# One hybrid decoder layer: the low part of k on both partition halves, and stick-breaking weights as products of sigmoids

## The chip, the core and the metric

The kernel runs on one NeuronCore of a Trainium2 chip. The metric is the device time of one execution in microseconds, lower is better. A NeuronCore has five engines that run their own instruction streams in order: TensorE (PE, with its weight loads shown apart as PEld), VectorE (DVE), ScalarE (ACT), GpSimd (POOL) and SyncE (SP), whose queue issues nearly all DMAs here. They wait for each other by semaphores.

## What is computed

One layer over 512 tokens of width 1024: a SwiGLU sublayer, a mixer of two attention groups side by side (8 heads of 64 each), and a second SwiGLU sublayer. Each is normed before and after and modulated by c. The change lies in the mixer:

```python
p = n @ w_in[l]
qa, ka, va, qi, ki, wi, qb, kb, vb = jnp.split(p, IN_SPLITS, axis=-1)
# group A: an indexer (8 heads qi, one shared ki) picks 128 keys a row; softmax over these
sc = relu(einsum('bthd,bsd->bths', qi, ki));  score = einsum('bths,bth->bts', sc, wi)
_, idx = lax.top_k(score, topk)
# group B: stick-breaking attention, strictly causal
z = jnp.einsum('bthd,bshd->bhts', qb, kb) * (D ** -0.5)
u = jnp.where(mask, jax.nn.log_sigmoid(-z), 0.0)
between = lax.cumsum(u, axis=3, reverse=True) - u
a = jnp.where(mask, jnp.exp(jax.nn.log_sigmoid(z) + between), 0.0)
```

So a[t,s] is sigmoid(z[t,s]) times the product of sigmoid(-z[t,j]) over s < j < t.

## The kernel before

All matrix products run on TensorE in its single-pass float32. To keep accuracy each operand is split into a high and a low part: `split` rounds the source to the high part (ACT, L132) and subtracts it from the source for the low part (DVE or POOL, L138). A projection is then three products per k-tile (L271 to L273: high times low, high times high, low times high), each of 128 rows and 512 columns.

The mixer runs in these stages:

- **Indexer.** `proj_block` (L293) and `proj` make the keys ki and four pairs of heads qi. Then come the scores: for each of 8 heads and token tiles 1 to 3, one q k^T (`qk`, L781) into a PSUM bank (tag `at`, three banks), a Relu on ACT (L734) into one of three buffers, and a weighted sum on DVE (L735).
- **Top-k.** Per row 16 rounds of MAX (L766) and MATCH_REPLACE (L769) on DVE, for three token tiles, then `ns` (L772). Nothing needs it before group A, and the scheduler strews it over DVE's stream among the work of group B.
- **Group B**, four units of two heads: `attn_b` makes the weights x, `transposed` turns them by PE and splits them (ACT, DVE), and `unit` multiplies them with v. Meanwhile `fill` issues the projection of the next unit's k, q and v, step by step.
- **Group A**, four units with `attn_a` in place of `attn_b`: a mask and bias table b (L917), the row maximum (L924), Exp (L927). The output projection's first products fill its last unit.

The order on each engine is fixed when the kernel is built, by a scheduler that goes by the program's order, buffers and its own costs.

How `qk` multiplies is what the first part of the change touches. q's two heads are stacked by `stack` (three SP DMAs of 64 partitions): head 0 has the tile [high; low], head 1 [low; high], and k is stacked as [high; high]. One product of 128 rows (L787) thus gives (q_high + q_low) k_high. The missing term q_high k_low is a product of its own ahead of it (L786), over the 64 partitions on which q_high of that head lies, with `kl`, the split's low part of k, which is not stacked.

`attn_b` per token tile of L = 128 to 512 keys: z in PSUM, with -1e30 added on the diagonal block (L893). ACT makes ln(1 + exp(-|z|)) in three steps (L895 to L897), ACT (tiles 0 and 1, L899) or DVE (tiles 2 and 3, L901) makes max(z, 0), DVE runs the sum of both from the right (the scan, L902), subtracts it from z (L903), and ACT takes Exp (L904). The function table of natural logarithm and exponential is loaded once, in the indexer (L685).

Of the kernel before, what the change touches and what calls it, by code (L numbers as in the profile page):

```python
# [20 lines left out]
S = 512  # L21
# [7 lines left out]
TOPK = 128  # L29
# [25 lines left out]
class Pools:  # L55
    """Work tiles of a phase: 4 KB ones (tag wk) have a pool of their own."""
# [8 lines left out]
class Block:  # L65
    """One launch's context: the tile pools that last, the constants and the parts of the layer."""
# [42 lines left out]
    # ---- pieces  # L109

    def w_load(self, src, view, n=1024, alloc=None, lo=None, hi=None):
        """A block of weights in SBUF, split."""
# [11 lines left out]
    def w_cols(self, w, c0, m, alloc=None, lo=None, hi=None):  # L124
        """Columns c0..c0+m of w [1024, n], as [128, 8, m], split."""
# [3 lines left out]
    def rounded(self, hi, src, eng=None):  # L129
        """src in the tensor engine's single-pass float32."""  # L130
# [4 lines left out]
    def split(self, hi, lo, src, eng=None, hi_eng=None):  # L135
        """src = hi + lo exactly, both in the tensor engine's single-pass float32."""
        a = self.rounded(hi, src, hi_eng)
        return a, (eng or self.nc.vector).tensor_sub(lo, src, hi.bitcast(F32))  # L138
# [36 lines left out]
    def ada_cols(self, m, k0, k1):  # L175
        """What follows from modulation m's columns k0..k1."""
# [11 lines left out]
    def gate_row(self, s, pool):  # L188
        """gate * g_post of sublayer s, on every partition."""
# [5 lines left out]
    def turn(self, src, nk, tp):  # L195
        """src [128 tokens, nk * 128] transposed, four k-tiles a bank."""
# [9 lines left out]
    def to_cols(self, banks, scale_col, shift_col, nh, i, pool):  # L206
        """The banks of turn() scaled and shifted, rounded into token tile i of nh; the rest of it for rest_cols()."""
# [21 lines left out]
    def norm_rows(self, i, pool):  # L229
        """h[i] times its reciprocal root mean square."""  # L230
# [13 lines left out]
    def pre_norm(self, s, n, tp, pool):  # L244
        """The stages of a pre-norm: rows, their transposes, columns."""
# [21 lines left out]
    def mm3(self, ps, w, n, k, m, cols):  # L267
        """The three products of k-tile k that make ps += (w n), w and n split."""
# [6 lines left out]
    def proj(self, w, c0, m, n, psum, lo=None):  # L275
        """(n w[:, c0:c0+m])^T as [m, S] in PSUM."""
# [6 lines left out]
    def proj_block(self, ws, n, banks, ends=()):  # L283
        """Several such products, over the first token tiles before the last ones, whose transposes come meanwhile."""
# [16 lines left out]
    def down_load(self, w, ks, n, half, alloc=None, lo=None):  # L301
        """Half the columns of w's k-tiles ks[n] and ks[n + 1], split: (n, high, low) of each."""
# [5 lines left out]
    def down_mms(self, ps, lhs, ks, i, ck):  # L308
        """Token tile i's products of the k-tiles ck; lhs(k): k-tile k's high and low parts, transposed."""
# [7 lines left out]
    def down(self, lhs, ks, w, g, banks, pool, alloc, stages, begun=0, out=None):  # L317
        """h += g * rmsnorm(lhs^T w), over the k-tiles ks in their order; then each token tile i goes
        through the stages. banks(half): four accumulators; the first half has begun k-tiles in them."""
# [61 lines left out]
    # ---- sublayers  # L381
# [582 lines left out]
```

## Time and profile before

| | |
|---|---|
| median of 3 runs | 1148.08 us (1143.62 to 1151.46) |
| the profiled execution | 1141.3 us from its first to its last instruction; what its own run took around that is not shown apart |
| PE busy | 1089.9 us (95%) |
| PEld busy | 871.1 us (76%) |
| DVE busy | 632.3 us (55%) |
| ACT busy | 434.9 us (38%) |
| POOL busy | 167.7 us (15%) |
| granted TensorE clock, mean | 0.991 of 2.4 GHz |

A busy PE is not yet a PE at its best: matmuls are pipelined, and their records overlap. What a product really costs is the step from its start to the next one's start. In the rows, L12 is line 12 of the kernel; `64*128 64x256` is a product with 64 rows of weights, 128 columns of them, over 256 columns of the other operand; `xN` is a count; in square brackets stand the engine's idle time just before and what ended it. `SPq` is an issue of DMAs.

### The profile page before, as it was taken

The page shows a single profiled execution, that of the slowest core. Times are in us where ns is not written, and L with a number is a line of the kernel's source. Part 1 is how long each engine was busy: PE and PEld are TensorE (multiplying, and loading weights), DVE is VectorE, ACT ScalarE, POOL GpSimd, SP SyncE. Part 2 cuts the span into 40 slices and gives each one's busy share as a digit, 9 for nine tenths or more (in the row PEclk, how much of TensorE's full clock was granted, in tenths as well). Part 3 has the DMA queues.
Part 4 walks back from the last instruction along what each step waited for, and adds up shares of the span by engine and source line. Part 5 has one row for each costly group of instructions (what it writes and reads, how often), then busy time and mean ns, then how long its engine had stood idle before and what let it go on. Part 6 is the DMA issues. An engine that isn't in the chain of part 4 may idle for free.

```text
span 1141.3 us, 13392 instructions
## 1 busy us (share of the span) xinstructions
PE 1089.9 (95%) x5079; PEld 871.1 (76%) x5079; DVE 632.3 (55%) x1055; ACT 434.9 (38%) x790; POOL 167.7 (15%) x116
## 2 busy tenths in 40 slices
PE   3889999999999999999999999989999999999997
PEld 2767888888888887667776677769888888888886
DVE  5979898834223184599999756474333333332313
ACT  3322222223213363477774645555232223321220
POOL 2110000000000433323323320423000000000030
PEclk9889999999999999999999999999999999999999
DMA  9967897732222504322234322412333333322321
GB/s 280 274 203 270 287 303 247 249 100 93 92 93 93 157 20 106 91 75 64 78 87 125 83 84 84 130 55 63 99 98 92 93 105 97 92 92 95 99 84 74
DMA packets 169444, 142.91 MB, mean 125 GB/s; under 512 B 6748, under 2 KB 142076, under 8 KB 169380
## 3 DMA queue, kind: packets, MB, share of 16 engines
q1 hardware_dynamic: 167872, 139.82, 40.2%
q10 hardware_dynamic: 1508, 2.24, 0.6%
q8 instruction: 40, 0.66, 0.2%
q14 instruction: 24, 0.20, 0.1%
HBM read 132.04 MB, written 2.13 MB: 118 GB/s over the span
## 4 chain that ended last, share of the span: by engine, by line
PE 79%; DVE 10%; issue 3%; ACT 2%; SPq 2%; DMA 2%; POOL 1%; DVEq 0%; POOLq 0%; ACTq 0%
PE mm L271 14%; PE mm L273 14%; PE mm L272 14%; PE mm L314 7%; PE mm L315 7%; PE mm L313 7%; PE mm L293 3%; PE mm L466 3%; PE at L787 2%; PE at L786 2%; DVE y L902 1%; DVE h L339 1%; SPq L420 1%; DVE tk L769 1%; PE tp L880 1%
## 5 line engine op out<-in xcount | busy, mean ns | idle before, releaser
L132 ACT ACTIVATE wh<-raw 128x1024 fp32r<-128x1024 f32 x156 | 164.3, 1057 | 450.4 <-PE mm L272 145.7
L271 PE MATMUL mm<-nl,wh 128*128 128x512 f32 x808 | 319.4, 395 | 0.0
L272 PE MATMUL mm<-nh,wh 128*128 128x512 f32 x808 | 316.5, 392 | 0.0
L273 PE MATMUL mm<-nh,wl 128*128 128x512 f32 x808 | 316.4, 392 | 0.0
L138 DVE TENSOR_TENSOR wl<-raw,wh 128x1024 fp32r<-128x1024 f32 (+1 forms) x116 | 142.3, 1227 | 223.3 <-ACT wh L132 223.2
L273 PEld LDWEIGHTS mm<-nh,wl 128*128 128x128 f32 x808 | 151.8, 188 | 30.9
L272 PEld LDWEIGHTS mm<-nh,wh 128*128 128x128 f32 x808 | 152.0, 188 | 28.7
L271 PEld LDWEIGHTS mm<-nl,wh 128*128 128x128 f32 x808 | 152.2, 188 | 28.4
L315 PE MATMUL mm<-wh,hT 128*128 128x512 f32 x352 | 138.6, 394 | 0.0
L314 PE MATMUL mm<-wh,hT 128*128 128x512 f32 x352 | 138.6, 394 | 0.0
L313 PE MATMUL mm<-wl,hT 128*128 128x512 f32 x288 | 113.6, 395 | 0.0
L138 POOL TENSOR_TENSOR wh<-raw,wh 128x1024 fp32r<-128x1024 f32 x10 | 25.5, 2558 | 595.0 <-ACT wh L132 591.8
L138 POOL TENSOR_TENSOR wl<-raw,wh 128x1024 fp32r<-128x1024 f32 x31 | 74.6, 2408 | 164.9 <-ACT wh L132 142.8
L514 DVE TENSOR_TENSOR sg<-sg,mm 128x512 f32<-128x512 f32 x44 | 30.1, 685 | 106.5 <-PE mm L273 91.5
L314 PEld LDWEIGHTS mm<-wh,hT 128*128 128x128 f32 x352 | 66.3, 188 | 15.3
L315 PEld LDWEIGHTS mm<-wh,hT 128*128 128x128 f32 x352 | 66.3, 188 | 15.1
L153 DVE SCALAR_TENSOR_TENSOR acc<-ra,sc,acc 128x1024 f32<-128x1024 f32 x49 | 62.8, 1281 | 5.6 <-DMA ra<-in_w_ada_dram 4.8
L313 PEld LDWEIGHTS mm<-wl,hT 128*128 128x128 f32 x288 | 54.3, 188 | 12.7
L466 PE MATMUL mm<-nh,wh 128*128 128x512 f32 x96 | 35.6, 450 | 6.8 <-ACT nh L445 6.8
L786 PE MATMUL at<-kq 64*128 64x256 f32 (+2 forms) x88 | 37.6, 427 | 2.8 <-DVE mx L924 2.0
L787 PE MATMUL at<-kq 128*128 128x256 f32 (+2 forms) x88 | 38.0, 432 | 0.0
L786 PEld LDWEIGHTS at<-kq 64*128 64x128 f32 x88 | 16.1, 183 | 27.4 <-issue 13.9
(213 smaller groups left out, 1358.1 us busy)
## 6 DMA issues: line engine op xcount, KB each, us to landing
ra<-in_w_ada_dram SPq DMA_DIRECT2D x56, 512.0 KB, 5.1
raw<-in_w_ffn_gate_dram SPq DMA_DIRECT2D x44, 512.0 KB, 3.7
raw<-in_w_ffn_up_dram SPq DMA_DIRECT2D x44, 512.0 KB, 3.7
raw<-in_w_ffn_down_dram SPq DMA_DIRECT2D x44, 512.0 KB, 3.4
raw<-in_w_in_dram SPq DMA_DIRECT2D x28, 512.0 KB, 3.8
ra<-in_w_ada_dram SPq DMA_DIRECT2D x32, 256.0 KB, 5.4
kq<-kq SPq DMA_DIRECT2D x60, 128.0 KB, 2.3
raw<-in_w_out_dram SPq DMA_DIRECT2D x8, 512.0 KB, 3.9
```

Of the source, the lines that this page charges most:

```text
L132: return self.nc.scalar.activation(hi, src, AF.Copy)
L138: return a, (eng or self.nc.vector).tensor_sub(lo, src, hi.bitcast(F32))
L153: nc.vector.scalar_tensor_tensor(acc, raw, sc[:, k:k + 1], acc, op0=ALU.mult, op1=ALU.add)
L271: nc.tensor.matmul(ps[0:m, c], w[0][:, k, :], n[1][:, k, c], start=k == 0, stop=False)
L272: nc.tensor.matmul(ps[0:m, c], w[0][:, k, :], n[0][:, k, c], start=False, stop=False)
L273: return nc.tensor.matmul(ps[0:m, c], w[1][:, k, :], n[0][:, k, c], start=False, stop=k == KD - 1)
L313: nc.tensor.matmul(ps, lh[:, t], wl, start=n == 0, stop=False)
L314: nc.tensor.matmul(ps, ll[:, t], wh, start=False, stop=False)
L315: nc.tensor.matmul(ps, lh[:, t], wh, start=False, stop=n == len(ks) - 1)
L466: nc.tensor.matmul(banks[j], ws[j][l][:, k, :], n[r][:, k, :], start=k + o == 0, stop=k == KD - 1 and o == 2)
L786: nc.tensor.matmul(ps, q[hd][b, t], kl[b, 0:n], start=True, stop=False)
L787: nc.tensor.matmul(ps, q[hd][:, t], k[hd][:, 0:n], start=False, stop=stop)
```

## The change

`qk` takes the low part of k for each head as a tile of its own, over all 128 partitions, so that its first product has 128 rows too; it now also adds q_low k_low. For this `end_k` stacks `kl` as it stacks `kh` (three DMAs and one tile more for each unit of two heads), and the tag `kq` gets 13 buffers in place of 12. In the indexer ki lies on both halves already. Room is made by a bf16 mask `cm` and by `kk` in the ring `w2`.

`attn_b` takes sigmoid(-z) and sigmoid(z) on ACT, runs the product of sigmoid(-z) from the right on DVE (a scan with a broadcast column of ones as its second operand), and multiplies sigmoid(z) with the product one place to the right. The table loaded in the indexer is that of sigmoid; the one with Exp is loaded later, ahead of group A's first Exp.

```diff
     def kq_tile(self, n=2):
-        return [self.upool.tile([128, 512], F32R, tag="kq", name="kq", bufs=12) for _ in range(n)]
+        return [self.upool.tile([128, 512], F32R, tag="kq", name="kq", bufs=13) for _ in range(n)]
...
-        cm = pool.tile([128, 512], F32, tag="cm", name="cm")
+        cm = pool.tile([128, 512], BF16, tag="cm", name="cm")
...
-        load = nc.scalar.preload_act_table_set("natural_log_exp_and_others")
+        load = nc.scalar.preload_act_table_set("sigmoid_and_others")
...
-            kk = pool.tile([128, NT, 64], F32, tag="kk", name="kk")
+            kk = pool.tile([128, NT, 64], F32, tag="w2", name="kk", bufs=3)
...
-                self.qk(ps, i, hd % 2, qi[hd // 2], (kih, kih), kil, True)
+                self.qk(ps, i, hd % 2, qi[hd // 2], (kih, kih), (kil, kil), True)
...
-        t, b = slice(i * 128, (i + 1) * 128), slice(64 * hd, 64 * hd + 64)
-        nc.tensor.matmul(ps, q[hd][b, t], kl[b, 0:n], start=True, stop=False)
+        t = slice(i * 128, (i + 1) * 128)
+        nc.tensor.matmul(ps, q[hd][:, t], kl[hd][:, 0:n], start=True, stop=False)
         nc.tensor.matmul(ps, q[hd][:, t], k[hd][:, 0:n], start=False, stop=stop)
...
         def end_k():
-            kh, st["kl"] = self.kq_tile()
-            self.split(kh, st["kl"], st["ps"])
+            kh, kl = self.kq_tile()
+            self.split(kh, kl, st["ps"])
             st["k"] = self.stack(kh, kh)
+            st["kl"] = self.stack(kl, kl)
...
-            nc.scalar.activation(xs, z, AF.Abs)
-            nc.scalar.activation(xs, xs, AF.Exp, scale=-1.0)
-            nc.scalar.activation(xs, xs, AF.Ln, bias=1.0)
-            if i < 2:
-                nc.scalar.activation(ys, z, AF.Relu)
-            else:
-                nc.vector.tensor_scalar(ys, z, 0.0, None, op0=ALU.max)
-            nc.vector.tensor_tensor_scan(ys[:, ::-1], ys[:, ::-1], xs[:, ::-1], 0.0, op0=ALU.add, op1=ALU.add)
-            nc.vector.tensor_sub(xs, z, ys)
-            nc.scalar.activation(xs, xs, AF.Exp)
+            nc.scalar.activation(ys, z, AF.Sigmoid, scale=-1.0)
+            nc.scalar.activation(xs, z, AF.Sigmoid)
+            nc.vector.tensor_tensor_scan(ys[:, ::-1], ys[:, ::-1], self.ones.to_broadcast([128, L]), 1.0,
+                                         op0=ALU.mult, op1=ALU.mult)
+            nc.vector.tensor_mul(xs[:, 0:L - 1], xs[:, 0:L - 1], ys[:, 1:L])
```

The scheduler also orders the mixer's work anew. Two places show it. First DVE at the end of group B; `tk` and `ns` belong to top-k, `pt` and `v` to a unit's products, `y` and `x` to `attn_b`. Before, the last of top-k stands behind the last weights of group B:

```order
L769 MATCH_REPLACE tk<-m_4912,tk 128x256
L769 MATCH_REPLACE tk<-m_4914,tk 128x384
L769 MATCH_REPLACE tk<-m_4916,tk 128x512
L772 TENSOR_TENSOR ns<-tk,sco 128x256
L772 TENSOR_TENSOR ns<-tk,sco 128x384
L138 TENSOR_TENSOR v<-tp,v 128x8x64
L867 TENSOR_TENSOR ob<-ob,tp 128x4x64
L772 TENSOR_TENSOR ns<-tk,sco 128x512
```

After the change, on the same engine and at the end of the same group, it stands ahead of the last head's weights (the first column of lines is that of the changed kernel: L899 is the scan, L901 the product):

```order
L772 TENSOR_TENSOR ns<-tk,sco 128x384
L138 TENSOR_TENSOR kq<-mm,kq 128x512
L138 TENSOR_TENSOR pt<-tp,pt 128x256
L899 SCALAR_TENSOR_TENSOR y<-y,ones 128x256
L772 TENSOR_TENSOR ns<-tk,sco 128x512
L901 TENSOR_TENSOR x<-x,y 128x255
L899 SCALAR_TENSOR_TENSOR y<-y,ones 128x384
L901 TENSOR_TENSOR x<-x,y 128x383
L899 SCALAR_TENSOR_TENSOR y<-y,ones 128x512
L901 TENSOR_TENSOR x<-x,y 128x511
```

What moved: top-k ends some ten instructions earlier in DVE's stream, with group B's last weights behind it. Second, SP's queue in one unit of group B, with k's stack, the weights `raw` of a later projection, and q's stack. Before (`kq_4600` is k's high part, `kq_4702` and `kq_4703` q's parts):

```order
L778 DMA kq_4604<-kq_4600 64x512 x2
L778 DMA kq_4600<-kq_4600 64x512
L120 DMA raw_5308<-in_w_in_dram 128x8x128
L778 DMA kq_4708<-kq_4702 64x512
L778 DMA kq_4708<-kq_4703 64x512
L778 DMA kq_4702<-kq_4703 64x512
L120 DMA raw_5400<-in_w_in_dram 128x8x128
```

After, in the same queue and unit (`kq_4529` and `kq_4530` are k's high and low parts, `kq_4626` and `kq_4627` q's):

```order
L778 DMA kq_4533<-kq_4529 64x512 x2
L778 DMA kq_4537<-kq_4530 64x512 x2
L120 DMA raw_5224<-in_w_in_dram 128x8x128
L778 DMA kq_4529<-kq_4529 64x512
L778 DMA kq_4530<-kq_4530 64x512
L120 DMA raw_5236<-in_w_in_dram 128x8x128
L778 DMA kq_4632<-kq_4626 64x512
L778 DMA kq_4632<-kq_4627 64x512
L778 DMA kq_4626<-kq_4627 64x512
L120 DMA raw_5332<-in_w_in_dram 128x8x128
```

What moved: three DMAs more stand with k's stack, ahead of the weights and of q's stack.

## Rows read from the trace of the kernel before

**Rows 1.** Busy us (xinstructions) of PE, PEld, DVE, ACT, POOL by stage; then PEclk, DMA share, GB/s
```profile
445.00:486.00 41.00, 41.00 (x154) 26.00 (x152) 21.73 (x25) 16.77 (x32) 14.34 (x8) 1.00 0.43 112
486.00:612.00 126.00, 124.67 (x593) 88.32 (x594) 121.89 (x272) 90.53 (x216) 37.92 (x20) 1.00 0.28 76
612.00:632.00 20.00, 17.60 (x83) 12.51 (x82) 15.67 (x44) 7.94 (x24) 3.61 (x3) 1.00 0.38 118
632.00:735.00 103.00, 98.63 (x483) 74.53 (x483) 63.14 (x162) 56.39 (x127) 32.74 (x18) 1.00 0.35 100
```
**Rows 2.** PE's waits from 445 to 735 us: total us, times, longest us
```profile
PE at L786 <- DVE mx L924: 2.0, 1, 2.0
PE tp L880 <- DVE pt L138: 2.0, 4, 1.4
...
PE at L786 <- DMA kq<-kq: 0.8, 1, 0.8
...
PE tp L863 <- ACT ot L860: 0.2, 1, 0.2
```
**Rows 3.** Timeline of the indexer, one pair of score products: start us, us, what
```profile
446.16 0.19 PEld L273 LDWEIGHTS mm<-nh,wl 128*128 128x128 f32 x1
446.39 0.39 PE L273 MATMUL mm<-nh,wl 128*128 128x512 f32 x1
446.70 0.18 PEld L786 LDWEIGHTS at<-kq 64*128 64x128 f32 x1 [0.36 <-issue]
446.70 0.38 PE L786 MATMUL at<-kq 64*128 64x256 f32 x1
447.01 0.19 PEld L787 LDWEIGHTS at<-kq 128*128 128x128 f32 x1
447.01 0.39 PE L787 MATMUL at<-kq 128*128 128x256 f32 x1
447.24 0.40 PE L271 MATMUL mm<-nl,wh 128*128 128x512 f32 x1
```
**Rows 4.** Timeline, the same around a pair of 512 columns, and L271 to L272
```profile
450.52 0.39 PE L273 MATMUL mm<-nh,wl 128*128 128x512 f32 x1
...
451.60 0.39 PE L271 MATMUL mm<-nl,wh 128*128 128x512 f32 x1
...
451.82 0.40 PE L272 MATMUL mm<-nh,wh 128*128 128x512 f32 x1
```
**Rows 5.** Timeline, eight products of 128 rows and 256 columns, and the next
```profile
425.86 1.12 PE L293 MATMUL mm<-nh,wl 128*128 128x256 f32 x8
426.82 0.28 PE L293 MATMUL at<-nh,wh 128*128 128x256 f32 x1
```
**Rows 6.** Busy us of L787 alone by stage: PE (xproducts), PEld
```profile
445.00:486.00 41.00, 10.63 (x24) 4.47 (x24) 1.00 0.43 112
486.00:612.00 126.00, 14.91 (x35) 6.51 (x35) 1.00 0.28 76
612.00:735.00 123.00, 12.48 (x29) 5.40 (x29) 1.00 0.35 103
```
**Rows 7.** DVE groups by line and form, 445 to 735 us: busy us, mean ns | idle before
```profile
L902 DVE TENSOR_TENSOR_SCAN y<-y,x 128x128 f32<-128x128 f32 x8 | 7.6, 945 | 0.1
L903 DVE TENSOR_TENSOR x<-at,y 128x512 f32<-128x512 f32 x8 | 5.4, 677 | 0.0
L901 DVE TENSOR_SCALAR y<-at 128x512 f32<-128x512 f32 x8 | 5.3, 669 | 0.3 <-ACT x L895 0.3
L138 DVE TENSOR_TENSOR wl<-raw,wh 128x1024 fp32r<-128x1024 f32 x4 | 4.9, 1220 | 1.7 <-ACT wh L132 1.7
L901 DVE TENSOR_SCALAR y<-at 128x384 f32<-128x384 f32 x8 | 4.3, 538 | 0.4 <-ACT x L895 0.4
```
**Rows 8.** Timeline: a POOL split, a scan beside it, and a scan with POOL idle
```profile
496.67 2.39 POOL L138 TENSOR_TENSOR wl<-raw,wh 128x1024 fp32r<-128x1024 f32 x1 [13.24 <-PE at L893]
...
497.99 1.35 DVE L902 TENSOR_TENSOR_SCAN y<-y,x 128x128 f32<-128x128 f32 x1
...
548.86 0.42 DVE L902 TENSOR_TENSOR_SCAN y<-y,x 128x128 f32<-128x128 f32 x1
```
**Rows 9.** Timelines of POOL, SP and PE where a unit begins: q's low part, its stack, its first use
```profile
539.99 1.30 POOL L138 TENSOR_TENSOR kq<-q,kq 128x512 fp32r<-128x512 f32 x1
540.85 4.36 SPq L778 DMA_DIRECT2D kq<-kq  x3
545.06 0.38 PE L786 MATMUL at<-kq 64*128 64x256 f32 x1
```
**Rows 10.** The page: DMAs of the stacks (KB each, us to landing), and ACT's table load
```profile
kq<-kq SPq DMA_DIRECT2D x60, 128.0 KB, 2.3
L685 ACT ACT_TABLE_LOAD x1 | 1.3, 1283 | 0.0
```

## The prediction

> **What bounds the kernel now.** The change touches only the mixer, so the first view is the busy time by stage [rows 1]. The stages are the indexer's scores (445 to 486 us), group B with top-k strewn in (486 to 612), the passage to group A (612 to 632) and group A (632 to 735). PE is busy all through: 41.00 of 41, 124.67 of 126, 17.60 of 20 and 98.63 of 103 us. In group B a second engine is full as well: DVE with 121.89 of 126 us. Elsewhere DVE has room (21.73 of 41, 63.14 of 103), and ACT has some everywhere (at most 90.53 of 126).
>
> The second view is PE's waits. From 445 to 735 us the list has nine rows, from 2.0 us down to 0.2 us, 7.7 us together [rows 2]. So PE seldom waits for another engine, and time is to be had from what PE does itself.
>
> The third view is the timeline around one score [rows 3]. A product of the projection loads its weights while the one before it runs: L273's load starts at 446.16, its product at 446.39, 0.23 us later. Not so around the product with 64 rows. Its load and its product both start at 446.70, 0.31 us behind the start of L273, after PEld had been idle for 0.36 us. The same happens to L787, back at 128 rows: load and product at 447.01. So PE does not load ahead when the number of rows changes, and each q k^T changes it twice.
>
> **Part 1, the low part of k on all 128 rows.** The cost of a pair now: from the start of the projection's product ahead of it to the start of the one behind it, 447.24 - 446.39 = 0.85 us at 256 columns [rows 3], and 451.60 - 450.52 = 1.08 us at 512 [rows 4]. The cost when all three have 128 rows: a product of 512 columns takes a step of 451.82 - 451.60 = 0.22 to 0.23 us [rows 4], one of 256 takes (426.82 - 425.86) / 8 = 0.12 us [rows 5]. That makes 0.23 + 2 x 0.12 = 0.47, and 3 x 0.23 = 0.69 us. The difference is 0.38 and 0.39 us, independent of the columns; I take 0.39. There are 24, 35 and 29 pairs in the three stretches of [rows 6], 88 in all: 9.4, 13.7 and 11.3 us, together 34.3 us of PE time. How much of it moves the end differs by stage.
>
> *Scores, 24 pairs.* PE sets the pace; DVE would have 21.7 us of work in 31.6. Bounds are 5 us (the last heads' scores stand close together, and there DVE's sums and the three `at` banks pace them) and 9.4 us. I take 7.5.
>
> *Group B, 35 pairs.* PE gives 13.7 us, but DVE is full too, so DVE decides, in part 2.
>
> *Passage, 5 of the last 29 pairs.* PE is idle for 2.4 us here already, waiting for DVE's table b and the row maximum [rows 1, 2]. I take 0; bounds -1 and 2 us.
>
> *Group A, 24 pairs.* 24 x 0.39 = 9.4 us. DVE and ACT are busy for less than two thirds. A faster PE will meet a few more waits for p and its split; I take 9, bounds 7 and 9.4.
>
> *The added stack.* Three more DMAs for each of 8 units, 24 of 128 KB; the like ones land 2.3 us after issue [rows 10]. What they could delay is q's stack, which is the late one: POOL starts q's low part at 539.99, the three DMAs are issued from 540.85 on, and PE uses the tile at 545.06 [rows 9]. The first two land by about 543.7 (540.85, some 0.6 us for the second issue, 2.3 us), 1.3 us ahead of use. The new DMAs stand ahead of q's, with k, a whole projection of q earlier (24 products of 0.23 us, 5.5 us, and attention work between). Two landings of 2.3 us fit into that, and the weights behind them are for a later projection. Cost 0, hidden by q's projection; without that cover it is up to 2.3 us a unit. The thirteenth buffer keeps six lasting tiles and one passing one of the next unit beside the six in use.
>
> **Part 2, sigmoids.** ACT drops from four or five passes per tile to two, and its chain from z to the weights from five steps behind each other to a sigmoid, a scan and a product. ACT bounds nothing, so this shortens latency that PE's other work hides; 0. One more table load of 1.28 us [rows 10] comes ahead of group A's first Exp, where ACT is busy for 7.94 of 20 us [rows 1]: 0, at most 1.3.
>
> DVE decides group B. It loses max(z, 0) for tiles 2 and 3: 8 x 0.669 + 8 x 0.538 = 9.7 us [rows 7]. The scan keeps its form with other operations; no row shows the product scan, and I take the same time. The subtraction (0.677 us at 512 columns, one operand in PSUM) becomes a product with both operands in SBUF. The nearest row with both in SBUF takes 1.220 us for 1024 columns, 0.61 for 512 [rows 7]; equal, then.
>
> But there is a price in [rows 8]. A scan of 128 keys takes 0.42 us with POOL idle, and 1.35 us when it starts at 497.99 inside a POOL split that runs from 496.67 to 499.06: it ends 0.28 us after it. The mean of the eight such scans is 0.945 us [rows 7], so (0.945 - 0.42) x 8 = 4.2 us of group B's DVE time are such delays. The Trainium skill, "SBUF — State Buffer", section "Who interferes with whom", states that a DVE instruction with two SBUF inputs and a GpSimd instruction that reads SBUF exclude each other for the whole instruction, and that one with a single SBUF input does not contend. The scan's row agrees. By that rule the change exposes 32 instructions that were safe. From the rows alone: 32 scans cost 4.2 us, so 32 more instructions of two SBUF operands may cost another 4.2 us. Bounds are 0 and all 32 delayed by the 1.35 - 0.42 = 0.93 us of [rows 8], 29.8 us. I take 4.2, since the same POOL splits run beside them.
>
> DVE's work in group B becomes 121.9 - 9.7 + 4.2 = 116.4 us. At the share it reaches now (121.89 of 126, 0.967) the stage takes 120.3 us, a gain of 5.7. With no delay it is 112.2 / 0.967 = 116.0, a gain of 10; PE alone would allow 13.7. Top-k now ends ahead of the last head's weights, so nothing is left behind them. I take 7.
>
> **The sum.** 7.5 + 7 + 0 + 9 = 23.5 us. The profiled execution's 1141.3 us become 1117.8. What lies around a span is not shown for that run; the three runs lie 2.3 to 10.2 us above it, their median 6.8. So the median goes from 1148.1 to 1148.1 - 23.5 = 1124.6, say 1124.5 us.
>
> **The rivals.**
>
> *PE alone decides.* Top-k only fills DVE's gaps, and its order is free enough that DVE keeps up. For it: PE's nine waits are short in group B too. Against it: DVE has 4 us left of 126. All 88 pairs pay: 1148.1 - 34.3 = 1113.8 us.
>
> *DVE's delays eat group B's gain.* Products wait for POOL often enough to take back the 9.7 us. Left are 7.5 + 9 = 16.5: 1131.6 us. For it: POOL is busy for 37.92 of 126 us. Against it: most scans start clear of it.
>
> *The rows are not the cause.* The gap around L786 would be the pair's own, from the PSUM bank or the issue, and remain with 128 rows. The Trainium skill, "TensorE: Matmul & The Clock Gate", section "LDWEIGHTS (loading the stationary operand)", says that a load's time goes by its columns and not its rows. The rows agree on the durations (0.18 and 0.19 us), and by that alone a product of 64 rows costs as much as one of 128 and part 1 brings nothing. Against this rival: L787 stays in L786's bank and starts late all the same, and L293's eight products of 128 rows go over into an `at` bank at their regular step [rows 5]. Left would be DVE's part, at most 5.7 us: about 1142 to 1148, say 1145.
>
> *Slower: every product waits for POOL.* The place is L901 after the change, the price 0.93 us each. DVE's work becomes 121.9 - 9.7 + 29.8 = 142.0 us, at 0.967 146.8, so group B grows by 20.8 us against 16.5 won elsewhere: 1148.1 + 4.3 = 1152.4. It decides from about 28 of the 32 products on (28 x 0.93 = 26 = 16.5 + 9.7). Against it: 4.2 us are four or five such delays among 32 scans.
>
> **How the numbers follow.** A measurement here tells about 1% from no change, 11.5 us. Chances: the forecast (1118 to 1129) 0.56; PE alone 0.20; delays eat group B 0.14; the rows not the cause 0.06; slower than before 0.04. The predicted time is the forecast's, 1124.5. The range 1110 to 1135 takes in the first three, with the runs' spread; outside stay the other two, and the tails. Faster by over 1% (below 1136.6): 0.56 + 0.20 + nearly all of 0.14, less a little for causes unseen: 0.87. Within 1%: the last two cases, mostly: 0.11. Slower by over 1%: 0.02.
>
> **What would show it.** Right: the weights of qk's first product load ahead of it, the pair with its neighbour steps 0.47 and 0.69 us instead of 0.85 and 1.08, 445 to 486 shrinks by 7 to 9 us, group A by about 9, and DVE stays over 95% busy in group B. Wrong: steps unchanged; a product on DVE whose mean is far above 0.68 us at 511 columns; PE waiting for `kq` DMAs or `pt` by more than some 8 us; a scan slower as a product; or DVE with large idle stretches in group B, which would speak for PE alone.

## The result and the profile after

| | before | after |
|---|---|---|
| median | 1145.85 us (4 runs, 1143.17 to 1151.46) | 1132.14 us (4 runs, 1131.17 to 1135.31) |
| the profiled execution | 1141.3 us | 1133.5 us, of a run of 1135.31 |

The ratio is 0.9875, with a 95% interval of 0.9831 to 0.9919: 1.25% faster (0.8 to 1.7%), 13.7 us. The forecast was 1124.5 us and a gain of 23.5. The two profiled executions are only 7.8 us apart, because the one of after is its slowest run and the one of before, at 1141.3 + 1.8, is about its fastest (1.8 us is what lies around the span of after). The steps below are read from these two.

Part 1 works as forecast. Timeline of after, a pair of score products (start us, us, what), as [rows 3]:

```profile
455.17 2.41 POOL L138 TENSOR_TENSOR wl<-raw,wh 128x1024 fp32r<-128x1024 f32 x1
455.42 2.44 DVE L735 SCALAR_TENSOR_TENSOR sco<-rl,wix,sco 128x256 f32<-128x256 f32 x1
...
456.19 0.39 PE L273 MATMUL mm<-nh,wl 128*128 128x512 f32 x1
456.19 0.19 PEld L787 LDWEIGHTS at<-kq 128*128 128x128 f32 x1
456.42 0.28 PE L787 MATMUL at<-kq 128*128 128x256 f32 x1
...
456.54 0.28 PE L788 MATMUL at<-kq 128*128 128x256 f32 x1
...
456.66 0.39 PE L271 MATMUL mm<-nl,wh 128*128 128x512 f32 x1
```

The weights of L787 load while L273 runs, and from L273 to L271 it takes 456.66 - 456.19 = 0.47 us, where it was 0.85. (The first two rows belong to the last section.)

The stages of after, as [rows 1]: scores, group B, passage, group A. Busy us (xinstructions) of PE, PEld, DVE, ACT, POOL; then PEclk, DMA share, GB/s:

```profile
445.00:480.00 35.00, 33.57 (x169) 28.23 (x167) 21.18 (x24) 16.18 (x32) 15.71 (x8) 1.00 0.53 136
480.00:600.00 120.00, 104.63 (x531) 80.89 (x532) 116.37 (x254) 57.21 (x127) 31.40 (x16) 0.97 0.33 86
600.00:620.00 20.00, 20.00 (x105) 15.82 (x104) 7.45 (x18) 9.33 (x20) 9.70 (x7) 1.00 0.54 154
620.00:723.00 103.00, 95.85 (x498) 78.16 (x497) 66.93 (x182) 59.83 (x137) 31.08 (x16) 0.98 0.38 109
```

In group B PE is busy for 104.63 of 120 us, where it had 124.67 of 126: 15 us of it are idle now. DVE is still full. Who PE waits for in after, 445 to 723 us (total us, times, longest), as [rows 2]:

```profile
PE tp L882 <- DVE x L901: 12.0, 12, 1.8
PE at L787 <- DMA kq<-kq: 3.8, 4, 1.3
PE tp L882 <- ACT p L924: 3.8, 4, 1.8
PE at L787 <- ACT rl L734: 1.7, 1, 1.7
PE at L787 <- DVE mx L921: 1.1, 1, 1.1
```

The first row is new: PE, about to turn the weights x, waits for DVE's product (L901), 12.0 us in group B. Two rows of before's list that [rows 2] leaves out, for x and for group A's p:

```profile
PE tp L880 <- ACT p L927: 0.5, 1, 0.5
PE tp L880 <- ACT x L904: 0.5, 2, 0.2
```

A stage table by PE's timeline fits all kernels: the scores, from the first q k^T to the first product with the diagonal mask (L895 in after); group B and the passage, from there to the first product with v in group A (L857); group A, from there to the last L293. What follows the start of the last L293 takes 335.4 us in each.

| us | first q k^T at | scores | B and passage | group A |
|---|---|---|---|---|
| before | 446.7 | 39.7 | 145.5 | 174.1 |
| after | 448.7 | 32.3 | 148.6 | 168.5 |
| difference | +2.0 | -7.4 | +3.1 | -5.6 |

Together -7.9, which is how far the two executions are apart, but for rounding. So in this pair the gap to the forecast, 15.6 us, lies in group B, which was to give 7 us and took 3.1, and in 3.4 us less from group A and 2.0 us ahead of the scores.

Not all of it is the change's. In after, four stretches of PE at its lower clock, some 1.7 us each (last section), fall between 440 and 655 us, and before has none there. It falls in other runs of before too: their mean clock goes down to 0.978 while their time goes up to 1156 us. By the medians the gap to the forecast is 9.8 us.

What DVE's instructions take in group B of after (busy us, mean ns | idle before), as [rows 7]; L899 is the scan, L901 the product:

```profile
L899 DVE TENSOR_TENSOR_SCAN y<-y,ones 128x512 f32<-128x512 f32 x8 | 9.7, 1206 | 0.0
...
L899 DVE TENSOR_TENSOR_SCAN y<-y,ones 128x256 f32<-128x256 f32 x8 | 7.3, 912 | 0.0
L899 DVE TENSOR_TENSOR_SCAN y<-y,ones 128x128 f32<-128x128 f32 x8 | 7.1, 892 | 0.0
...
L901 DVE TENSOR_TENSOR x<-x,y 128x255 f32<-128x255 f32 x8 | 4.8, 598 | 0.0
L901 DVE TENSOR_TENSOR x<-x,y 128x127 f32<-128x127 f32 x8 | 4.3, 543 | 0.0
```

A product of 127 columns takes longer on average than one of 383 (540 ns), a scan of 128 keys as long as one of 256: as in [rows 7, 8], some of them wait for POOL. The timeline of the last head in after shows what that does (start us, us, what [idle before <- releaser]):

```profile
589.20 2.90 POOL L138 TENSOR_TENSOR wl<-raw,wh 128x1024 fp32r<-128x1024 f32 x1 [9.85 <-ACT wh L132]
590.70 1.95 DVE L899 TENSOR_TENSOR_SCAN y<-y,ones 128x256 f32<-128x256 f32 x1
...
593.15 0.41 DVE L901 TENSOR_TENSOR x<-x,y 128x255 f32<-128x255 f32 x1
...
593.91 0.38 PE L882 MATMUL tp<-ident,x 128*128 128x128 f32 x2
...
595.15 0.55 PE L882 MATMUL tp<-ident,x 128*128 128x128 f32 x3 [0.86 <-DVE x L901]
...
596.33 0.69 DVE L901 TENSOR_TENSOR x<-x,y 128x511 f32<-128x511 f32 x1
...
597.08 0.55 PE L882 MATMUL tp<-ident,x 128*128 128x128 f32 x3 [1.15 <-DVE x L901]
```

The scan of 256 keys starts inside POOL's split and ends at 592.65, 0.55 us behind its end; everything behind it in DVE's queue is late, and PE waits twice for x, 0.86 and 1.15 us.

### The profile page after: what moved, and what is told of

Same layout as the page of the kernel before. It is cut to its first block, busy times and chain, and to the rows that moved or that the text cites. A ratio compares the mean times of both kernels' runs of the same rounds, so it can differ in the third digit from the quotient of the medians.

```text
span 1133.5 us, 13329 instructions
## 1 busy us (share of the span) xinstructions
PE 1064.6 (94%) x5079; PEld 874.3 (77%) x5079; DVE 625.6 (55%) x1039; ACT 407.0 (36%) x711; POOL 169.1 (15%) x116
## 3 DMA queue, kind: packets, MB, share of 16 engines
HBM read 132.04 MB, written 2.13 MB: 118 GB/s over the span
## 4 chain that ended last, share of the span: by engine, by line
PE 75%; DVE 15%; issue 4%; DMA 2%; ACT 2%; POOL 1%; SPq 0%; DVEq 0%; POOLq 0%; ACTq 0%
PE mm L271 13%; PE mm L273 13%; PE mm L272 13%; PE mm L314 7%; PE mm L315 7%; PE mm L313 7%; PE mm L293 3%; PE mm L466 3%; DVE y L899 2%; DMA ra<-in_w_ada_dram 2%; DVE x L901 1%; DVE tk L769 1%; DVE b L914 1%; DVE m L766 1%; PE tp L882 1%
## 5 line engine op out<-in xcount | busy, mean ns | idle before, releaser
L271 PE MATMUL mm<-nl,wh 128*128 128x512 f32 x808 | 320.2, 396 | 0.0
L272 PE MATMUL mm<-nh,wh 128*128 128x512 f32 x808 | 317.0, 392 | 0.0
L273 PE MATMUL mm<-nh,wl 128*128 128x512 f32 x808 | 316.9, 392 | 0.0
L273 PEld LDWEIGHTS mm<-nh,wl 128*128 128x128 f32 x808 | 152.2, 188 | 31.1
L272 PEld LDWEIGHTS mm<-nh,wh 128*128 128x128 f32 x808 | 152.5, 189 | 29.2
L271 PEld LDWEIGHTS mm<-nl,wh 128*128 128x128 f32 x808 | 152.7, 189 | 28.8
L313 PEld LDWEIGHTS mm<-wl,hT 128*128 128x128 f32 x288 | 54.3, 188 | 12.7
L787 PE MATMUL at<-kq 128*128 128x256 f32 (+2 forms) x88 | 30.7, 353 | 6.6 <-DMA kq<-kq 3.8
L138 DVE TENSOR_TENSOR pt<-tp,pt 128x512 fp32r<-128x512 f32 (+1 forms) x48 | 27.2, 595 | 13.7 <-ACT pt L132 13.5
L132 ACT ACTIVATE hT<-sg 128x512 fp32r<-128x512 f32 x44 | 27.8, 632 | 17.1 <-DVE sg L514 17.1
```

What stands on the lines that cost most here:

```text
L132: return self.nc.scalar.activation(hi, src, AF.Copy)
L271: nc.tensor.matmul(ps[0:m, c], w[0][:, k, :], n[1][:, k, c], start=k == 0, stop=False)
L272: nc.tensor.matmul(ps[0:m, c], w[0][:, k, :], n[0][:, k, c], start=False, stop=False)
L273: return nc.tensor.matmul(ps[0:m, c], w[1][:, k, :], n[0][:, k, c], start=False, stop=k == KD - 1)
L313: nc.tensor.matmul(ps, lh[:, t], wl, start=n == 0, stop=False)
L787: nc.tensor.matmul(ps, q[hd][:, t], kl[hd][:, 0:n], start=True, stop=False)
```

## The experiments

Each median below was taken beside runs of the kernel before on the same chip, whose medians were 1148.5 to 1149.9 us.

**First theory: top-k's tail.** After the result I took the tail of top-k for the cause: the scheduler had moved its last steps from behind the last weights, where DVE has room (7.45 of 20 us busy), into group B. Four runs tested it.

Part 1 alone, that is the kernel before with the edits to `qk`, `end_k` and the tiles, and with `attn_b` and its table as they were:

```diff
-        nc.tensor.matmul(ps, q[hd][b, t], kl[b, 0:n], start=True, stop=False)
+        nc.tensor.matmul(ps, q[hd][:, t], kl[hd][:, 0:n], start=True, stop=False)
...
+            st["kl"] = self.stack(kl, kl)
```

> The kernel before with the first part of the change alone (low part of k on all 128 rows); attn_b keeps its exponentials, and top-k's last 17 steps stay behind group B's last weights. Theory (top-k's tail, moved ahead of the last weights, takes DVE time in group B, where DVE has none): this kernel has the tail where it was, so group B shrinks by what DVE's 4 us of slack allow, 2 to 4 us; the scores by 7, group A by 6: about 1130 us, as fast as the whole change or a little faster. Rival (delays of the new products beside POOL's splits eat the gain): there are no such products here, but max(z, 0) is back with 9.7 us; group B about as before, 1131 to 1133. Rival (PE alone decides): 34 us less, 1112.

1122.53 us, ratio 0.9773 (0.9740 to 0.9807). Scores 32.3, B and passage 140.7, group A 165.7 us. Part 1 alone gives more than the whole change. PE's waits (440 to 740 us):

```profile
PE tp L881 <- DVE pt L138: 3.5, 7, 0.9
...
PE tp L881 <- ACT x L905: 1.5, 6, 0.4
```

Hardly any wait for x. This agrees with the tail theory in its direction only; that gave about 1130 us, 7.5 more than measured. For the rival of the delays I had reckoned 1131 to 1133, since it charged max(z, 0) in full; that charge was wrong, as the run with half of top-k shows.

Part 2 alone, with `qk` as before:

```diff
-        load = nc.scalar.preload_act_table_set("natural_log_exp_and_others")
+        load = nc.scalar.preload_act_table_set("sigmoid_and_others")
...
+            nc.scalar.activation(ys, z, AF.Sigmoid, scale=-1.0)
+            nc.scalar.activation(xs, z, AF.Sigmoid)
...
+            nc.vector.tensor_mul(xs[:, 0:L - 1], xs[:, 0:L - 1], ys[:, 1:L])
```

> The kernel before with the second part of the change alone (sigmoids and products); q k^T keeps its 64 rows, and top-k's tail stands ahead of the last weights as after the whole change. Theory (the moved tail): DVE loses 9.7 us of max(z, 0) in group B, and gets 9.6 us of tail and about 5 us of delays beside POOL: slower by 0 to 5 us, 1146 to 1151. Rival (PE alone decides): no change within 1 us, 1146. Rival (part 2 is worth the 5.7 us that the prediction gave it): 1140.

1150.34 us, ratio 1.0013 (0.9993 to 1.0033): no gain. B and passage take 155.1 us instead of 145.5, but PE's mean clock there is 0.96 in this profile, against 1.00, which is up to 6.2 of the 9.6 us. With part 1 in place, part 2 costs: 1132.14 us against the 1122.53 of part 1 alone.

The tail put behind the last weights:

```diff
-            nc.vector.tensor_mul(xs[:, 0:L - 1], xs[:, 0:L - 1], ys[:, 1:L])
+            self.last_mul = nc.vector.tensor_mul(xs[:, 0:L - 1], xs[:, 0:L - 1], ys[:, 1:L])
...
-                        for step in top:
+                        for step in top[:-15]:
                             step()
+                        with tc.issue_after(self.last_mul.ins):
+                            for step in top[-15:]:
+                                step()
```

> The changed kernel with the last 15 steps of top-k (about 8.5 us of DVE) issued behind group B's last product, where DVE has 12 idle us of 20; all else is the same code. Theory (the moved tail): group B ends some 8 us sooner, and the top-k that is left fits into the passage: 1122 to 1125 us, against 1132 of the changed kernel. Rival (delays of the products beside POOL, or the DMAs of the stacks, hold group B): DVE's work of 8.5 us less in group B helps, too, but waits for POOL and for DMAs stay: 1129 to 1132. Rival (what counts is the end of top-k, which group A waits for): the end of top-k moves behind the last weights, b comes later: 1132 or slower.

1131.77 us, against 1132.14: nothing. The tail is not the cause.

Half of top-k:

```diff
-        return [top, drop] * (TOPK // 8) + [lambda: nc.vector.tensor_tensor(ns, st["wk"], s, op=ALU.is_equal)]
+        return [top, drop] * (TOPK // 16) + [lambda: nc.vector.tensor_tensor(ns, st["wk"], s, op=ALU.is_equal)]
```

> The changed kernel with 8 of the 16 rounds of top-k for each token tile; half of the picking is left out, so group A sees other keys, and DVE has some 27 us less in group B. Theory (DVE sets group B's pace): group B is now PE's, 35 pairs x 0.39 = 13.7 us shorter than before the change instead of 3 us longer: 17 us from the changed kernel, 1115 us. Rival (PE's clock at half for some stretches, DMAs of the stacks, or PE's own steps hold group B): 1130 to 1132, no change from the changed kernel.

1129.15 us, 3.0 us less. The windows of group B, from its first mask product to the products with v of its last head, in after and in this kernel (columns as above):

```profile
480.90:595.40 114.50, 100.77 (x512) 77.75 (x511) 112.37 (x249) 55.23 (x122) 31.40 (x16) 0.97 0.33 86
```

```profile
480.40:589.00 108.60, 97.30 (x511) 75.54 (x510) 90.52 (x176) 54.94 (x122) 30.91 (x16) 1.00 0.34 87
```

DVE has 21.9 us less to do, and is idle for 18 of 108.6 us; yet the stage is 5.9 us shorter only, and PE still waits 9.3 us for x. So it is not the amount of DVE's work that holds group B. Both this theory and the prediction's "DVE decides" fall here. (The scheduler also set the last two units in another order here, with 6 products between z and the turnings of the even heads where after has 8; that may hide a part of the gain, hardly the rest of the 17 us that the theory gave.)

**Second theory: PE's order.** A turning is the transposition of a block of x by PE; it needs the finished x. What PE has to do between a head's last z and the turnings covers the time in which ACT and DVE make x; one fill step is six products of the projection. In the program of after 6 to 10 of the projection's products stand between a head's last z and the first turning of its last tile; before, and with part 1 alone, 16 to 20. The scheduler takes the new chain for shorter and calls the turnings sooner. Four runs tested that.

More products as cover: 12, by two fill steps behind a head's last tile, and 18, with a 3 in place of the 2:

```diff
             nc.vector.tensor_mul(xs[:, 0:L - 1], xs[:, 0:L - 1], ys[:, 1:L])
-            self.fill()
+            self.fill((1, 1, 1, 2)[i])
```

> The changed kernel with two fill steps in place of one behind the last token tile of each head's attn_b, so that 12 of the projection's products, not 6, stand between the last z and the turning of the weights. New theory (PE's order: the scheduler leaves 6 products there after the change and had 8 to 11 before the fourth turning, while the chain from z over sigmoid, scan and product takes 4 to 5 us, because DVE runs other steps in between): PE's waits for x fall from 12.0 us to 1 to 4 us, the drops of its clock in group B go with them, 1119 to 1124 us. Rival (DVE's full stage, delays beside POOL and top-k included, sets group B's length whatever PE's order): DVE has the same work, the wait moves to other places: 1130 to 1133.

1129.65 us, ratio 0.9822 (0.9793 to 0.9852). 2.5 us, not 8 to 13: PE waits 9.0 us for x, 6 times and up to 2.5, and 5.5 us for pt, its split.

The one with 18:

> The same with three fill steps behind the last token tile: 18 products (18 x 0.23 = 4.1 us) cover the chain. PE's order: waits for x near 0, 1116 to 1122 us; but the fill steps are used up sooner, and less is left to cover the products with v and the turning of the outputs, so it may give 1 to 3 us back against 12 products. DVE's full stage: 1130 to 1133.

1132.28 us: nothing.

12 products and the tail behind, the edits of both:

> 12 products of cover and, at once, the last 15 steps of top-k (about 8.5 us of DVE) behind group B's last product. If PE's order alone holds group B, the tail changes nothing, as it did with 6 products (1131.77 against 1132.14): within 1.5 us of the kernel with 12 products. If DVE is the bound once PE's waits are covered, the tail behind gains here what it did not there: 4 to 8 us faster than the kernel with 12 products.

1127.95 us; the tail adds 1.7 us to the 12 products, near to the 1.5 us that the theory allows and far from 4 to 8.

Part 1 alone with early turnings:

```diff
-        pts = [self.transposed(attn(hd, (qkv["q"], qkv["k"], qkv["kl"]))) for hd in range(2)]
+        qk = qkv["q"], qkv["k"], qkv["kl"]
+        pts = [self.transposed(attn(0, qk))]
+        with self.tc.issue_after(self.first_bank) if attn == self.attn_b else ExitStack():
+            p = attn(1, qk)
+        pts.append(self.transposed(p))
...
-            self.fill(3)
+            with self.tc.issue_after(self.first_bank) if attn == self.attn_b else ExitStack():
+                self.fill(3)
...
```

> The first part of the change alone, with exponentials as before, but in group B the first eight turnings of the weights are made to stand behind 6 products (the projection's and the next head's are issued after the fourth turning), as after the whole change. PE's order: the gain of part 1 in group B goes, with PE waits for x of 1.2 to 2.5 us a head, 8 heads: 1122.5 + 9 to 18 = 1132 to 1140 us. Rival (the products of the sigmoids are what costs the time: delays beside POOL, the scan of products, DVE's in-order queue): with exponentials the early turnings cost little, 1122 to 1126.

1155.05 us, ratio 1.0046 (1.0026 to 1.0066), 32.5 us more than part 1 alone. PE's waits:

```profile
PE tp L886 <- ACT x L912: 22.4, 13, 2.2
PE tp L886 <- DVE pt L138: 2.6, 2, 2.4
```

So the order of PE matters, even more than I expected, for the long chain of exponentials. Up to 19 of the 32.5 us are PE's clock, 0.973 in the mean of these runs against 0.989 with part 1 alone (1155 x 0.027 less 1123 x 0.011). But cover did not help the sigmoids. In the trace of the version with 12 products, three products of 511 columns take 2.13 to 2.45 us instead of 0.67, each beside a POOL split, and just there PE waits for x up to 2.5 us. These are all its delays, (1.303 - 0.674) x 8 = 5.0 us by the mean of the eight; after has 9.2, as the next run shows. So the 2.5 us that this version gained need not be the cover's. That led to the next runs.

**Third theory: waits of DVE for POOL, on the path.**

Operands in PSUM:

```diff
-        y = pool.tile([128, 1280], F32, tag="p", name="y", bufs=3)
...
-            nc.scalar.activation(ys, z, AF.Sigmoid, scale=-1.0)
             nc.scalar.activation(xs, z, AF.Sigmoid)
-            nc.vector.tensor_tensor_scan(ys[:, ::-1], ys[:, ::-1], self.ones.to_broadcast([128, L]), 1.0,
+            nc.scalar.activation(z, z, AF.Sigmoid, scale=-1.0)
+            nc.vector.tensor_tensor_scan(z[:, ::-1], z[:, ::-1], self.ones.to_broadcast([128, L]), 1.0,
                                          op0=ALU.mult, op1=ALU.mult)
-            nc.vector.tensor_mul(xs[:, 0:L - 1], xs[:, 0:L - 1], ys[:, 1:L])
+            nc.vector.tensor_mul(xs[:, 0:L - 1], xs[:, 0:L - 1], z[:, 1:L])
```

> The changed kernel with sigmoid(-z) and its running product kept in z's PSUM bank, so that neither the scan nor the product has two operands in SBUF; top-k, fill steps and the place of the turnings in the code are as after the change (the scheduler puts 10 to 12 products before the fourth tile's turning in the even heads instead of 6 to 10). Theory (delays beside POOL: after the change 5 scans and 2 products are longer by 9.6 us together): these delays vanish, and as DVE and PE's waits for x stand on one path, 4 to 9 us are won: 1123 to 1128 us. Rival (PE's order alone): the instructions keep their mean, waits for x stay at 8 to 12 us: 1130 to 1133. The delays may also stay if the operands' place does not matter: then the means of both lines stay as they are.

1121.21 us, ratio 0.9766 (0.9730 to 0.9803): 10.9 us less than after. DVE's groups, L898 the scan, L900 the product:

```profile
L898 DVE TENSOR_TENSOR_SCAN at<-at,ones 128x256 f32<-128x256 f32 x8 | 5.5, 691 | 0.0
...
L898 DVE TENSOR_TENSOR_SCAN at<-at,ones 128x128 f32<-128x128 f32 x8 | 3.4, 420 | 0.0
L900 DVE TENSOR_TENSOR x<-x,at 128x255 f32<-128x255 f32 x8 | 3.2, 406 | 0.0
L900 DVE TENSOR_TENSOR x<-x,at 128x127 f32<-128x127 f32 x8 | 2.2, 274 | 0.0
```

All delays are gone, though POOL's splits run on. Against these means, after lost (0.912 - 0.691 + 0.892 - 0.420) x 8 = 5.5 us in scans and (0.598 - 0.406 + 0.543 - 0.274) x 8 = 3.7 us in products, 9.2 together. PE's wait for x, and the window of group B:

```profile
PE tp L882 <- DVE x L900: 3.3, 7, 0.9
```

```profile
480.20:582.50 102.30, 96.96 (x511) 76.94 (x510) 99.71 (x238) 54.45 (x122) 30.90 (x16) 0.98 0.35 91
```

DVE works 12.7 us less here than after and group B is 12.2 us shorter; with half of top-k it worked 21.9 us less, for 5.9. It counts where DVE's time goes: the delays lie between z and x, top-k need not. PE's mean clock does not explain the gain: 0.987 to 0.990 in the runs of both.

The turnings written out in a better order:

```diff
...
+        turn0 = self.turns(x0, pt0)
+        x1 = self.attn_b(1, qk, lambda i: next(turn0, None) if i else None)
+        turn1 = self.turns(x1, pt1)
+        ps0 = pv(0, pt0)
+        self.fill()
+        next(turn1)
+        next(turn1)
+        self.fill()
+        next(turn1)
+        out(0, ps0)
...
```

> The changed kernel with group B's turnings written out in another order, near to the one that the first part alone has: head 0's three banks of turnings stand behind the first, second and third tile of head 1 (18, 24 and 30 products behind the last z), head 1's behind the products of head 0 with v and two fill steps. Theory (PE's order leaves too little between z and the turnings, and turnings in one clump leave nothing between them and the products with v): waits for x fall below 4 us, waits for pt below 2: 1118 to 1123 us. Rival (DVE's full stage): 1127 to 1131, as with 12 products of cover.

1136.17 us, ratio 0.9890 (0.9850 to 0.9930): a miss, slower than after if anything. PE's waits for x fall to 0.2 us, as expected, but it waits for pt, DVE's split of the turned weights, instead:

```profile
PE at L883 <- DVE pt L138: 9.1, 8, 1.5
...
PE tp L925 <- DVE pt L138: 3.6, 3, 1.4
```

DVE is late (its scans are still delayed, up to 2.30 us for 256 keys), and another order of PE only moves the place where that shows: 12.9 us of waits for x and pt, against 12.0 for x in after. That it is even slower goes with PE's clock, 0.983 in the mean of its six runs against 0.988 in after: some 6 us (1136 x 0.017 less 1132 x 0.012). PE's order as the sole cause falls.

This order and all operands in PSUM, the edits of both:

> Both: the strewn turnings and the operands in PSUM. If each cause is real and the strewn order does not already cover the delays, 1 to 4 us faster than the strewn turnings alone: 1115 to 1120 us. If PE is the bound once the turnings are strewn, the delays beside POOL are covered: within 1 us of the strewn turnings alone. If neither is the cause: 1127 to 1132.

1119.58 us, ratio 0.9750 (0.9710 to 0.9791). With the delays gone, nearly the same order is 16.6 us faster than with them (some 7 us of it by PE's clock, 0.989 in the mean of its runs against 0.983), and 1.6 us faster than the operands in PSUM alone, which the intervals don't separate. It is the fastest kernel here.

Only the product's operand in PSUM:

```diff
-            nc.vector.tensor_tensor_scan(ys[:, ::-1], ys[:, ::-1], self.ones.to_broadcast([128, L]), 1.0,
+            nc.vector.tensor_tensor_scan(z[:, ::-1], ys[:, ::-1], self.ones.to_broadcast([128, L]), 1.0,
                                          op0=ALU.mult, op1=ALU.mult)
-            nc.vector.tensor_mul(xs[:, 0:L - 1], xs[:, 0:L - 1], ys[:, 1:L])
+            nc.vector.tensor_mul(xs[:, 0:L - 1], xs[:, 0:L - 1], z[:, 1:L])
```

> The changed kernel with the running product written into z's PSUM bank: the product (32 instructions) then reads one operand from PSUM, as the subtraction did before the change, while the scan still has both operands in SBUF. PE's order is within a product or two of the version with all operands in PSUM (1121.21 us). Theory (delays beside POOL, both lines): the products' delays, 3.7 us after the change, vanish, the scans' 5.8 us stay: about 1126 to 1129 us. If the products' delays alone cost the time, as the one thing that the change newly exposed: 1120 to 1123. If only the scans' do: 1130 to 1133.

1126.15 us, ratio 0.9803 (0.9764 to 0.9843), at the near edge of what the theory gave. One split of POOL shows both cases, L901 the product and L899 the scan:

```profile
582.84 2.47 POOL L138 TENSOR_TENSOR wl<-raw,wh 128x1024 fp32r<-128x1024 f32 x1 [10.93 <-ACT wh L132]
...
583.86 0.41 DVE L901 TENSOR_TENSOR x<-x,at 128x255 f32<-128x255 f32 x1
584.19 1.94 DVE L899 TENSOR_TENSOR_SCAN at<-y,ones 128x384 f32<-128x384 f32 x1
```

The product with one operand in PSUM runs through in 0.41 us; the scan with both in SBUF, started 0.33 us later, takes 1.94 us (0.956 in the version with all operands in PSUM) and ends 0.82 us behind the split.

| | delays of scan and product | PE's waits for x | median |
|---|---|---|---|
| after | 9.2 us | 12.0 us | 1132.14 us |
| product's operand in PSUM | 4.8 us | 7.7 us | 1126.15 us |
| both in PSUM | 0 | 3.3 us | 1121.21 us |

(4.8: the means of the scans of 128 and 384 keys are 903 and 1073 ns, against 420 and 956.) From after to the product in PSUM, 4.4 us of delays go with 6.0 us of time; from there to both in PSUM, 4.8 us with 4.9. So a microsecond of delay costs about one at the end, or a little more.

There are three reserves. PE's order moves too: these two versions have 10 to 12 products ahead of the even heads' last turnings and 6 to 8 products with v ahead of the odd heads', where after has 8 to 10 and 1 to 5. And a wait of ACT goes: in after x and y share three buffers, so that x of a unit's second head waits for DVE's last product of the first, which still reads y (480 to 600 us):

```profile
ACT x L898 <- DVE x L901: 5.2, 4, 1.5
```

With the product in PSUM this is 0.7 us, and without y it is gone. Both lie in the step from after to the product in PSUM; the step from there to both in PSUM has nearly one order and only the 0.7 us, and it gives the 4.9 us all the same. Last, the versions ran on four chips, and after not again beside them. Before's medians there lie 1.4 us apart, so a difference of one or two us between versions shows nothing.

## Why the prediction was right, and where it was not

The time, 1132.14 us, lies in the range, and the kernel is faster by over 1%, as most likely; the gain is little more than half of the forecast. That the time lies inside is owed to the width of the range, which took in a rival with 0.14; the mechanism of the forecast for group B failed.

*Scores:* forecast 7.5 us, measured 7.4, and 32.3 us in each version with part 1. Right, and so is the cause, the rows of weights.

*Passage and group A:* forecast 0 and 9. Group A gave 5.6, and 8.4 with part 1 alone. The 5.6 lie outside the bounds of 7 and 9.4. The gap is in the "few more waits for p": 3.8 us for p in after, against 0.5, and a stretch of PE at half its clock (last section). The added table load, which I had put at 0, was not hidden either:

```profile
L924 ACT ACT_TABLE_LOAD x1 | 1.3, 1283 | 2.8 <-DVE nm L923 2.8
```

It began only when the row maximum was there, and put off group A's first Exp by 1.28 us. How much of the waits for p comes from it, no run shows.

*The stack:* four waits for `kq` DMAs, 3.8 us together, against 0.8 [rows 2]. Forecast 0, with 2.3 us a unit without cover; it stayed below the 8 us that I had named as wrong.

*Group B:* the term that failed. The size of the delays was about right: 4.2 + 4.2 forecast, 5.5 + 3.7 measured. So was the loss of the 9.7 us of max(z, 0). The failed step is the one that turned them into time: "DVE decides group B", its work divided by the share 0.967. This made a microsecond saved anywhere on DVE worth as much as one lost anywhere. With half of top-k DVE's work fell by 21.9 us for 5.9 us of group B, 3.0 us at the end; without the delays, 9.2 us of them gave 10.9. Full as it was, DVE could put off top-k; it could not put off the chain from z to x, on which PE waits. And I priced that chain at 0, as "latency that PE's other work hides": before, 16 to 20 of the projection's products stood behind the last z; in the order of after there were 6 to 10, and the order, unlike the times, was known. The gain of max(z, 0) went, since it shortened what could wait anyway; the delays came to the end in full. Two smaller faults: by its own sum the gain with delays was 5.7 us, and it took 7; and it left out the tail of top-k, about 8.5 us of DVE, that the new order moves into group B. The run with the tail put behind shows that the latter cost nothing (1131.77).

*The rivals:* the one at 1131.6 us, DVE's delays eat group B's gain, gave the mechanism, except that more of the delays are the scans' than the products'. That its time is met within 0.6 us is in part luck: it has 0 for group B and 9 for group A, where the profiles show 3.1 us lost and 5.6 won, and it starts from a median of before that came out 2.2 us lower. I gave it 0.14 for the reason "most scans start clear of it"; that counted how often they collide and not where. The Trainium skill ("SBUF — State Buffer", "Who interferes with whom") states that a DVE instruction with two SBUF inputs and a GpSimd one that reads SBUF exclude each other, and that one with a single SBUF input, outside the two-port modes, does not contend. The traces agree: 0.41 against 1.94 us beside one split, and all seven late scans and products of after lie beside one. PE alone decides (1113.8) is out: PE is idle for 15 of 120 us of group B. That every product waits for POOL is out as well: those of 383 and 511 columns take 540 and 674 ns in after, none longer than undisturbed. That the rows are not the cause fell with the 0.47 us. The Trainium skill ("TensorE: Matmul & The Clock Gate", "LDWEIGHTS (loading the stationary operand)") states that a load's time goes by its columns and not by its rows. The durations still agree, 0.18 and 0.19 us [rows 3], but this is about the load's length and not about whether it runs ahead.

The start of the scores, 2.0 us later, was in no step, and no run shows it to be the change's: kernels with the same indexer start them between 446.2 and 451.1 us, the five latest with PE's clock at its lower level from about 440 us on. What stays open: how much of the lead of part 1 alone over the whole change is its wider order and how much its smaller delays (2.6 us, by the mean of 749 ns of its scans of 128 keys); and how much the freed buffer and the moved order add to the gain of the versions in PSUM. To move POOL's splits away was not tried.

## What to carry to other kernels

Where an instruction of DVE gets a second operand in SBUF in place of PSUM, look for POOL work at the same time, and for who waits for that instruction: a delay on the chain that PE waits for came to the end in full here, while 21.9 us saved elsewhere on DVE gave 3.0. An engine that is 97% busy need not be the bound if part of its work can be put off; the test is to take that part away. And a change that makes a chain shorter by the scheduler's reckoning also takes away the work that it put behind it, so count the covering work in the new order.

## What the runs showed of the hardware

PE's granted clock fell after stretches in which PE had idled, but not after each of them. Windows of after, columns as above:

```profile
440.00:445.00 5.00, 4.72 (x27) 4.67 (x27) 2.92 (x8) 1.61 (x3) 0.17 (x1) 0.66 0.52 134
495.00:500.00 5.00, 2.94 (x16) 2.01 (x15) 5.00 (x8) 0.93 (x2) 0.56 (x1) 0.94 0.58 155
500.00:505.00 5.00, 5.00 (x22) 4.32 (x22) 3.99 (x12) 2.72 (x5) 0.10 (x1) 0.72 0.02 5
560.00:565.00 5.00, 2.59 (x14) 1.62 (x13) 5.00 (x11) 0.16 (x1) 0.00 (x0) 0.93 0.79 210
565.00:570.00 5.00, 5.00 (x22) 4.20 (x21) 3.99 (x11) 2.98 (x6) 0.37 (x1) 0.73 0.00 0
```

From 495 to 500 us PE was busy for 2.94 of 5 us, and the mean clock was 0.94 and then 0.72 of 2.4 GHz; the same from 560 on. At the lower of its two levels, 1.2 GHz, PE loses (0.06 + 0.28) x 5 = 1.7 us each time, an estimate. At that level eight products of 128 rows and 256 columns take 444.26 - 442.56 = 1.70 us, at the upper one 0.96 [rows 5]:

```profile
442.56 1.91 PE L293 MATMUL mm<-nl,wh 128*128 128x256 f32 x8
444.26 1.97 PE L293 MATMUL at<-nh,wh 128*128 128x256 f32 x13
```

After has four such drops from 440 to 655 us, before has none from 445 to 735 [rows 1]. But before idled as long just ahead of that, and its clock stayed:

```profile
435.00:440.00 5.00, 2.23 (x18) 1.82 (x17) 3.87 (x9) 1.50 (x5) 3.43 (x2) 1.00 0.41 105
440.00:445.00 5.00, 5.00 (x44) 4.95 (x44) 2.99 (x6) 2.66 (x4) 1.28 (x1) 1.00 0.61 154
```

So a wait of PE can cost more than its own length.

The exclusion also holds for another form: the weighted sum of the scores (L735, two operands in SBUF and a scalar), in the first rows of the result, takes 2.44 us beside POOL's split, 0.47 elsewhere, and ends 0.28 us behind it. The running product costs DVE what the running sum did (1206 ns for 512 keys; 1215 for the sum, with part 1 alone).
